# The up product of an MLP as seven products of halves, with the residual kept in DRAM meanwhile

## The chip, the cores and the metric

The program runs on one core of one Trainium2 chip. The metric is the device time of one execution in microseconds (us); of the kernel before, three runs took 4327.98, 4333.91 and 4335.40 us, so the median is 4333.91 us. A profile of one further execution was taken.

The engines by the names that the profile uses: PE multiplies matrices into PSUM, PEld loads its stationary operand, DVE (VectorE) and ACT (ScalarE) work on tiles and may read PSUM, POOL (GpSimd) works on tiles in SBUF alone, SP issues DMAs. ACT issues DMAs as well.

## The reference, cut to what matters

Two layers of a transformer block run on 1024 tokens with 1024 features; a second, larger layer follows them. The end of each of the two layers is the part that changes:

```python
x = x + gate_a * mix                                   # mix = mixed @ w_out
h = rms_norm(x) * (1.0 + scale_f) + shift_f
x = x + gate_f * (jnp.square(jax.nn.relu(h @ w_mlp_up[l])) @ w_mlp_down[l])   # 1024 -> 4096 -> 1024
```

In the second layer's filters, `h @ w4` (64 features, 2 x 512 channels per direction) is multiplied by a decay; that is where the last part of the change is.

## The kernel before, in words

Activations lie transposed: a tile `x[f, hf]` holds 128 features (f of 8) by 512 tokens (hf of 2), and a matmul has 512 columns. All matrix products are in three parts for precision: each fp32 operand is split into a high part (`split_hi`, L194, a copy on ACT that rounds) and a low part (`split_lo`, L200, a subtraction on POOL or DVE), and high*high, high*low and low*high are accumulated in PSUM. A split of a tile of 128x1024 serves a block of weights of 1024x128.

`lighter` (L1317) picks DVE or POOL for a tile operation by adding up fixed costs, 0.60 for DVE and 1.23 for POOL for 512 columns; `plus` (L1326) uses it.

Order of work. The program is written in Python; when it is built, a list scheduler gives every engine one fixed queue. It takes instructions by their place in the program (earlier is more urgent) as soon as its own model of time says that they are ready and a buffer is free. On the chip each engine then works through its queue in that order and waits at each instruction for its semaphores. A buffer tag with `bufs=2` has two tiles in turn; a third must wait until the first is free.

The end of a layer, `layer1` from L559: the output projection (`project_out`, L579) adds `w_out` products to `xa`. Its last part, for the second half of the tokens, runs after the norm of the first half, with 2 PSUM tiles (tag `mm`). `norm` (L291) takes the sum of squares (`presum`, `rstd`) and makes, from each `xa[f, hf]`, a scaled tile (L299, DVE), a shift (ACT) and the split: DVE and ACT for f in 0, 2, 4, 6, 7, and ACT and POOL for f in 1, 3, 5. The split features H (16 tiles, high and low) stay for the up product, and `xa` stays as residual.

`mlp` (L605), up stage: 16 quarters (c of 8, j of 2). A quarter loads two blocks of `w_mlp_up` of 1024x128 (columns 256 apart), splits them, and makes 2 x 2 products of 24 matmuls (`up_part`, L617): 96 matmuls. ACT takes the ReLU out of PSUM (L622), DVE multiplies (L623). `up_store` (L633) writes the four results and, for c < 7, three more combinations (four subtractions on DVE, L640 to L646) to DRAM, on the ACT queue: they are the factors of the down product, which is made already as seven products of halves for c < 7 (`factor`, L688; `multiply`, L720). Its first weights are split before the up stage ends. `gated` (L733) adds to `xa`. Then the next layer's norm begins.

`filter_spectra` (L1500) makes, for pairs of 128 positions, four products in fp32 with 64 rows of the PE: direction b of 2 lies in rows 0 to 63 or 64 to 127 and writes its own PSUM bank, e is the position block. Each product is two matmul instructions. They stand in the order b0 e0, b0 e1, b1 e0, b1 e1.

Of the kernel before, what the change touches and what calls it, by code (L numbers as in the profile page):

```python
# [19 lines left out]
NF = D // 128  # L20
# [127 lines left out]
class Kernel:  # L148
# [319 lines left out]
    def layer1(self, l, state, xclose, enter_next, rclose):  # L468
        nc, i = self.nc, self.i
        _, H, xs, close = state  # L470
# [7 lines left out]
        mixd = self.DR.tile([2, 8, 2, 128, 512], F32, name=f"mix{l}")  # L478
# [4 lines left out]
        tmp, tclose = self.open("mla_tmp", "right")  # L483
# [12 lines left out]
        with self.pool("mod") as p:  # L496
# [14 lines left out]
            for n in range(34):  # L511
                h, i = divmod(n, 8)
# [19 lines left out]
        rclose()  # L532

        xp, xclose = self.open("x", "right")
        xa = {(f, hf): xp.tile([128, 512], F32, name=f"xa{f}_{hf}") for hf in range(2) for f in range(NF)}
        gp0, gclose0 = self.open("gla_in", "right")
        G = self.gla_setup(l, gp0, A)
        self.psum(f"ps_gla{l}")
# [21 lines left out]
        self.psum(f"ps_mlp{l}")  # L560

        mp, mpclose = self.open("mlp", "right")
        hp, hclose = self.open("h2_0")
        hq, hqclose = self.open("h2_1")
        H = {}
        self.h_tiles(H, hp, "f", 0)
        self.h_tiles(H, hq, "f", 1)
        s1 = self.C.tile([128, NF], F32, name=f"s1_f{l}")
        nc.vector.tensor_scalar(s1, scale_f, 1.0, None, op0=ALU.add)
        with self.pool("ntmp2", "left") as tmp:  # L570
            for hf in range(2):
                if hf:
                    self.drain(self.project_out(l, mp, mixd, 0, xa, gate_a, "mm", 2, (hf,)))
                self.norm(tmp, xa, H, s1, shift_f, hf)
        mpclose()
        return self.mlp(l, H, xa, gate_f, lambda: (hqclose(), hclose()), lambda: enter_next(xa, wclose)), xclose

    def project_out(self, l, mp, mixd, part, xa, gate, tag, bufs, halves=(0, 1)):

# [22 lines left out]
        for _ in steps:  # L602
            pass

    def mlp(self, l, H, x, gate, hclose, enter_next):  # L605


        nc, i = self.nc, self.i
        up, down = i["w_mlp_up"][l], i["w_mlp_down"][l]

        actd = self.DR.tile([8, 7, 2, 128, 512], F32, name=f"act{l}")
        dp, dpclose = self.open("mlp_raw", "right")
        sp, spclose = self.open("mlp_sq")

        def square():
            return sp.tile([128, 512], F32, name="square", tag="square", bufs=11)

        def up_part(w, hf):
            ps = self.PS.tile([128, 512], F32, name="up", tag="dn", bufs=4)
            self.gemm(ps, w, slice(0, 128), lambda k, h: H[k, h], 8, hf)  # L620
            sq = square()
            nc.scalar.activation(sq, ps, AF.Relu)  # L622
            nc.vector.tensor_mul(sq, ps, sq)  # L623
            return sq

        def up_weights(c, j):
            return [self.load_w([(up[:, n0 : n0 + 128], 0)], 8, 128, shared="v" if c + j == 0 else False) for n0 in (c * 512 + j * 128, c * 512 + j * 128 + 256)]

        def up_store(c, j, B):

            store = lambda n, t: nc.scalar.dma_start(actd[c, n, j], t)
            if c == 7:
                for n in range(4):  # L633
                    store(n, B[n // 2, n % 2])
                return
            store(0, B[0, 0])
            store(1, B[1, 0])
            store(2, B[1, 1])
            t2, t3, t4 = square(), square(), square()
            nc.vector.tensor_sub(t3, B[1, 1], B[0, 1])  # L640
            store(6, t3)
            nc.vector.tensor_sub(B[0, 1], B[0, 1], B[0, 0])
            store(4, B[0, 1])
            nc.vector.tensor_sub(t2, B[1, 1], B[0, 1])
            store(5, t2)
            nc.vector.tensor_sub(t4, B[1, 0], t2)  # L646
            store(3, t4)

        def raw_a(c, m, k):
# [7 lines left out]
        def raw_b(c, n):  # L657
            t = dp.tile([128, 2, 512], F32, name="sq_raw", tag="sqr", bufs=5)
            nc.sync.dma_start(t, actd[c, n].rearrange("j p n -> p j n"))
            B[c, n] = t  # L660

        turns = {}

        def exact(name, raw, lo_vector=False):

# [53 lines left out]

        def multiply(f, pairs):  # L720

            turns["ps"] = (turns.get("ps", -1) + 1) % 3
            tag, bufs = ("mm", 2) if turns["ps"] == 2 else ("dn", 4)
            ps = self.PS.tile([128, 512], F32, name="dn", tag=tag, bufs=bufs)
            n, last = 0, 6 * len(pairs) - 1
            for (wh, wl), (ah, al) in pairs:
                for j in range(2):
                    for a, b in ((wh, ah), (wh, al), (wl, ah)):
                        self.mm(ps, a[:, j, f * 128 : f * 128 + 128], b[:, j], n == 0, n == last)
                        n += 1  # L730
            return ps
# [2 lines left out]
            nc.vector.scalar_tensor_tensor(x[f, hf], y, gate[:, f : f + 1], x[f, hf], op0=ALU.mult, op1=ALU.add)  # L734

        load = loads()
        for c in range(8):
            for j in range(2):
                w, sq = up_weights(c, j), {}
                if (c, j) == (7, 1):  # L740

                    next(load)
                    next(load)
                    first = factor(0, 0)
                    next(first)
                    next(first)

                for m, hf in ((0, 0), (1, 0), (0, 1), (1, 1)) if c + j == 0 else ((0, 0), (0, 1), (1, 0), (1, 1)):
                    sq[m, hf] = up_part(w[m], hf)
                up_store(c, j, sq)  # L750
        spclose()
        hclose()
        dx, dxclose = self.open("mlp_late", "right")
# [749 lines left out]
    def filter_spectra(self, p, o, g):  # L1503

        nc, n = self.nc, 256
        if o + g == 0:
            self.mats = p.tile([128, 25, 128], F32, name="dftf")
        dec_ = self.k["decay"].rearrange("p (b a c) -> p b a c", b=2, a=8)[:, :, :, g * n : (g + 1) * n]
        ze = p.tile([128, 8, n], F32, name="ze", tag="ze", bufs=1)
        zo = p.tile([128, 8, n], F32, name="zo", tag="zo", bufs=1)  # L1510
        for a in range(0, 8, 2):
            dec = p.tile([128, 2, 2, n], F32, name="decay", tag="decay", bufs=2)
            for b in range(2):
                nc.sync.dma_start(dec[:, b], dec_[:, b, a : a + 2])
            ps = self.PS.tile([128, 2, 2, n], F32, name="f_ps", tag="big", bufs=2)
            for b in range(2):
                P = slice(64 * b, 64 * b + 64)
                for e in range(2):
                    self.mm(ps[:, b, e], self.hid[P, (a + e) * 128 : (a + e + 1) * 128], self.fw4[P, o, g * n : (g + 1) * n], True, True)
                self.load[0] += 0.67  # L1520
                nc.vector.tensor_mul(dec[:, b], ps[:, b], dec[:, b])
            self.plus(ze[:, a : a + 2], dec[:, 0], dec[:, 1])
            self.plus(zo[:, a : a + 2], dec[:, 0], dec[:, 1], ALU.subtract)
        slots = {}

        def Y(d):
            slots[d] = p.tile([128, 2, n], F32, name="Yf", tag="Yf", bufs=4)
            return slots[d]

        def flush(ds):  # L1530
            for d in ds:
# [715 lines left out]
```

## Time and profile before

| what | value |
|---|---|
| median of three runs | 4333.91 us |
| the profiled execution's own time | 4335.62 us |
| its span, first to last instruction | 4333.8 us |
| mean granted clock of PE | 0.963 |
| PE busy | 4008.1 us (92%) |
| DVE, ACT, POOL busy | 2228.9, 1529.8, 1590.5 us |
| up stage, layer 0 and 1 | 713.6 to 1072, 2064.9 to 2421 us |

Busy time is the time in which at least one instruction of the engine is shown; the matmuls overlap (each is shown with some 390 ns, and the next one starts after some 227 ns), so the rate of PE is read from the number of matmuls in a stretch. In a line of a view, `out<-in` names tiles by the program's names.

### The profile page before, as it was taken

The numbers are of one execution on the slowest core, as the hardware profiler recorded it, in microseconds if no ns is written. First come the engines' busy times: TensorE is split into PE (matmuls) and PEld (weight loads), VectorE is DVE, ScalarE is ACT, GpSimd is POOL, SyncE is SP. The second block draws the span as 40 slices with busy tenths as digits, with TensorE's granted clock in tenths as the row PEclk, the third lists the DMA queues.
The fourth block names the chain that finished last, engine by engine and source line by source line (L and its number), as shares of the span: only waits on it lengthen the run. The fifth ranks groups of instructions, "written<-read, shape, count | busy, mean of one in ns | idle before, by whom it ended". The sixth has DMA issues, their size and how long they took to land. (4 is left out here: it accounts for less than half of the span.)

```text
span 4333.8 us, 52750 instructions
## 1 busy us (share of the span) xinstructions
PE 4008.1 (92%) x19412; PEld 3134.3 (72%) x19412; DVE 2228.9 (51%) x3919; ACT 1529.8 (35%) x2774; POOL 1590.5 (37%) x1315
## 2 busy tenths in 40 slices
PE   6999888999999899888999999899999999999698
PEld 3776676888787595566788788567777776778576
DVE  5426686332788516586433477742221444567445
ACT  5425454212433525444311333322223545211222
POOL 3422364222876422165222688212220111334242
PEclk8999899999999999999999999999999999999899
DMA  6245534433442126643433443344454332444363
GB/s 199 61 132 170 161 113 141 162 134 122 161 156 81 48 86 197 193 132 112 161 132 133 151 145 106 108 106 116 117 144 96 98 93 79 143 148 145 127 180 109
DMA packets 634355, 563.12 MB, mean 130 GB/s; under 512 B 202536, under 2 KB 473854, under 8 KB 634098
## 3 DMA queue, kind: packets, MB, share of 16 engines
q1 hardware_dynamic: 412826, 409.31, 31.2%
q10 hardware_dynamic: 220696, 149.27, 10.9%
q8 instruction: 153, 2.51, 0.2%
q0 software_dynamic: 576, 1.18, 0.1%
q14 instruction: 104, 0.85, 0.1%
HBM read 399.49 MB, written 157.54 MB: 129 GB/s over the span
## 5 line engine op out<-in xcount | busy, mean ns | idle before, releaser
L200 POOL TENSOR_TENSOR w_lo<-w_raw,w_hi 128x1024 fp32r<-128x1024 f32 (+4 forms) x237 | 447.7, 1890 | 1458.6 <-ACT w_hi L194 1401.5
L194 ACT ACTIVATE w_hi<-w_raw 128x1024 fp32r<-128x1024 f32 (+4 forms) x276 | 236.6, 859 | 800.7 <-PE in L191 283.4
L191 PE MATMUL in<-b2h,w_hi 128*128 128x512 f32 x1152 | 474.9, 412 | 7.1 <-ACT qkv_t L1794 7.1
L191 PE MATMUL in<-b2l,w_hi 128*128 128x512 f32 x1152 | 460.2, 400 | 0.6 <-POOL b2l L200 0.6
L191 PE MATMUL in<-b2h,w_lo 128*128 128x512 f32 x1152 | 460.5, 400 | 0.0
L191 PE MATMUL up<-fl,w_hi 128*128 128x512 f32 x1024 | 400.3, 391 | 1.9 <-POOL fl L200 1.2
L191 PE MATMUL up<-fh,w_hi 128*128 128x512 f32 x1024 | 400.7, 392 | 0.0
L191 PE MATMUL up<-fh,w_lo 128*128 128x512 f32 x1024 | 400.2, 391 | 0.0
L191 PE MATMUL dn<-b_hi,a_hi 128*128 128x512 f32 x912 | 358.7, 395 | 4.2 <-ACT b_hi L194 2.0
L191 PE MATMUL dn<-b_lo,a_hi 128*128 128x512 f32 x912 | 359.0, 394 | 2.6 <-POOL b_lo L200 2.6
L191 PE MATMUL dn<-b_hi,a_lo 128*128 128x512 f32 x912 | 358.9, 394 | 0.0
L623 DVE TENSOR_TENSOR square<-up,square 128x512 f32<-128x512 f32 x128 | 88.2, 691 | 460.7 <-ACT square L622 452.8
L200 POOL TENSOR_TENSOR a_lo<-dn_raw,a_hi 128x1024 fp32r<-128x1024 f32 x92 | 241.1, 2621 | 119.2 <-ACT a_hi L194 119.0
L191 PEld LDWEIGHTS in<-b2h,w_hi 128*128 128x128 f32 x1152 | 221.6, 192 | 66.7 <-issue 13.1
L191 PEld LDWEIGHTS in<-b2h,w_lo 128*128 128x128 f32 x1152 | 221.2, 192 | 54.1 <-issue 7.3
L191 PEld LDWEIGHTS in<-b2l,w_hi 128*128 128x128 f32 x1152 | 221.5, 192 | 48.5 <-issue 4.4
L200 POOL TENSOR_TENSOR b_lo<-sq_raw,b_hi 128x1024 fp32r<-128x1024 f32 x92 | 239.5, 2604 | 6.2 <-ACT b_hi L194 6.2
L194 ACT ACTIVATE a_hi<-dn_raw 128x1024 fp32r<-128x1024 f32 x106 | 112.6, 1062 | 338.8 <-PE dn L191 118.3
L191 PE MATMUL wo<-mix,w_hi 128*128 128x512 f32 x512 | 185.4, 437 | 43.0 <-DVE xa L598 26.2
L191 PEld LDWEIGHTS up<-fl,w_hi 128*128 128x128 f32 x1024 | 192.9, 188 | 44.3 <-POOL fl L200 2.1
L191 PEld LDWEIGHTS up<-fh,w_hi 128*128 128x128 f32 x1024 | 193.2, 189 | 41.6 <-issue 0.8
L191 PEld LDWEIGHTS up<-fh,w_lo 128*128 128x128 f32 x1024 | 193.1, 189 | 40.5 <-issue 0.5
(505 smaller groups left out, 8721.0 us busy)
## 6 DMA issues: line engine op xcount, KB each, us to landing
wada<-in_w_ada SPq DMA_DIRECT2D x120, 512.0 KB
act<-square ACTq DMA_DIRECT2D x212, 256.0 KB
sq_raw<-act SPq DMA_DIRECT2D x106, 512.0 KB
w_raw<-in_w_in SPq DMA_DIRECT2D x102, 512.0 KB
w_raw<-in_w_mlp_up SPq DMA_DIRECT2D x64, 512.0 KB
dn_raw<-in_w_mlp_down SPq DMA_DIRECT2D x64, 512.0 KB
qkv<-qkv_t ACTq DMA_DIRECT2D x72, 256.0 KB
w_raw<-in_w_out SPq DMA_DIRECT2D x64, 256.0 KB
```

The source lines that it names most:

```text
L191: return self.nc.tensor.matmul(out, lhsT, rhs, start=start, stop=stop, **kw)
L194: self.nc.scalar.activation(hi, x, AF.Copy, **kw)
L200: return eng.tensor_sub(lo, x, hi.bitcast(F32))
L623: nc.vector.tensor_mul(sq, ps, sq)
```

## The change

1. **Up product.** A quarter's weights are taken as blocks a11, a12 (first 128 columns; first and last 512 features) and a21, a22 (second 128 columns), and the features as b11, b21 (first half of the tokens; first and last 512 features), b12 and b22. Sums of blocks are made and split, and seven products of 12 matmuls with 512 features each replace the four of 24: 84 matmuls a quarter. The results are put together by additions out of PSUM on DVE, with one copy on ACT; ReLU and square are one DVE instruction in SBUF. Per quarter the weights need four sums on DVE and six splits (one of 1024 columns, five of 512).
2. **Features.** The normed features are written in place, into `xa`; for the second half of the tokens, 4 x 4 differences and 4 x 5 splits on `lighter`'s choice of DVE or POOL make the factors of the products 2 to 6. 40 tiles stay in `h2`, 16 more lie in the place of `xa`.
3. **Residual.** `xa` is written to DRAM on the ACT queue (16 DMAs per layer) before the norm overwrites it, and read back on SP (16 DMAs) when the places are free, before the down product adds to it.
4. **Differences for the down product.** The four subtractions of `up_store` go from DVE to POOL; results and differences lie in pairs in the buffers of the down stage's `sq_raw` (5 of them).
5. **Order.** The first products of the first two quarters, which need the first half of the tokens alone, stand ahead of all the rest.
6. **Output projection.** Its last part uses 4 PSUM tiles (tag `dn`) in place of 2.
7. **Filters.** The four products of a pair stand in the order e0 b0, e0 b1, e1 b0, e1 b1, held by explicit dependencies.

The core of the diff:

```diff
+        xd = self.DR.tile([NF, 2, 128, 512], F32, name=f"x_mlp{l}")
+        H = {(q, f): [hp.tile([128, 512], F32R, name=f"f{q}{b}{f}") for b in "hl"] for q in (0, 1, 2, 4, 6) for f in range(4)}
+        def exact(q, f, t):
+            self.split_hi(H[q, f][0], t)
+            self.split_lo(H[q, f][1], t, H[q, f][0], True)
         with self.pool("ntmp2", "left") as tmp:
             for hf in range(2):
                 if hf:
-                    self.drain(self.project_out(l, mp, mixd, 0, xa, gate_a, "mm", 2, (hf,)))
-                self.norm(tmp, xa, H, s1, shift_f, hf)
+                    self.drain(self.project_out(l, mp, mixd, 0, xa, gate_a, "dn", 4, (hf,)))
+                r = self.norm_rstd(tmp, xa, hf)
+                for f in range(NF):
+                    nc.scalar.dma_start(xd[f, hf], xa[f, hf])
+                for f in range(4):
+                    for g in (f, 4 + f):
+                        t = xa[g, hf]
+                        nc.vector.scalar_tensor_tensor(t, t, s1[:, g : g + 1], r, op0=ALU.mult, op1=ALU.mult)
+                        nc.scalar.activation(t, t, AF.Identity, bias=shift_f[:, g : g + 1])
+                    if hf == 0:
+                        exact(0, f, xa[f, 0])
+                        exact(1, f, xa[4 + f, 0])
+                        continue
+                    b11, b12, b21, b22 = xa[f, 0], xa[f, 1], xa[4 + f, 0], xa[4 + f, 1]
+                    exact(2, f, b22)
+                    self.plus(t3, b22, b12, ALU.subtract)
+                    exact(6, f, t3)
+                    self.plus(b12, b12, b11, ALU.subtract)
+                    exact(4, f, b12)
+                    self.plus(t2, b22, b12, ALU.subtract)
+                    self.plus(t4, b21, t2, ALU.subtract)
+                    H[5, f] = [place(f, 0, F32R), place(f, 1, F32R)]
+                    exact(5, f, t2)
+                    H[3, f] = [place(4 + f, 1, F32R), place(4 + f, 0, F32R)]
+                    exact(3, f, t4)
...
+        def up_quarter(c, j):
...
+            w0 = pair("w")
+            split(w0, 0, R[0], c + j == 0)
+            p1 = temp("p1", 2)
+            nc.scalar.activation(p1, up_product(0, part(w0, 0)), AF.Copy)
+            c11, c21 = squares()
+            V.tensor_add(c11, up_product(1, part(w0, 1)), p1)
+            V.scalar_tensor_tensor(c11, c11, 0.0, c11, op0=ALU.max, op1=ALU.mult)
+            yield
+            w2 = pair("w")
+            split(w2, 0, a22)
+            V.tensor_add(a22, a21, a22)
+            V.tensor_sub(a21, a11, a21)
+            V.tensor_sub(a11, a22, a11)
+            V.tensor_sub(a12, a12, a11)
+            w1 = pair("a")
+            split(w1, 0, a11)
+            split(w1, 1, a21)
+            split(w2, 1, a22)
+            w3 = pair("w" if last else "b")
+            split(w3, 0, a12)
+            yield
+            V.tensor_add(u2, up_product(5, part(w1, 0)), p1)
+            V.tensor_add(u3, up_product(6, part(w1, 1)), u2)
+            yield
+            V.tensor_add(c21, up_product(3, part(w2, 0)), u3)
+            V.scalar_tensor_tensor(c21, c21, 0.0, c21, op0=ALU.max, op1=ALU.mult)
+            ps = up_product(4, part(w2, 1))
+            V.tensor_add(c22, ps, u3)
+            V.tensor_add(u4, ps, u2)
+            V.scalar_tensor_tensor(c22, c22, 0.0, c22, op0=ALU.max, op1=ALU.mult)
+            V.tensor_add(c12, up_product(2, part(w3, 0)), u4)
+            V.scalar_tensor_tensor(c12, c12, 0.0, c12, op0=ALU.max, op1=ALU.mult)
+            up_store(c, j, {(0, 0): c11, (0, 1): c12, (1, 0): c21, (1, 1): c22})
...
-            t2, t3, t4 = square(), square(), square()
-            nc.vector.tensor_sub(t3, B[1, 1], B[0, 1])
+            (t2, t3), (t4, _) = squares(), squares()
+            minus = nc.gpsimd.tensor_sub
+            minus(t3, B[1, 1], B[0, 1])
...
+        for n in range(2):
+            next(quarters[n])
...
+        for t in (1, 0):
+            for f in range(NF):
+                x[f, t] = place(f, t)
+                nc.sync.dma_start(x[f, t], xd[f, t])
...
+            group = []
+            for e in range(2):
+                for b in range(2):
+                    P = slice(64 * b, 64 * b + 64)
+                    group.append(self.mm(ps[:, b, e], self.hid[P, ...], self.fw4[P, o, ...], True, True))
+            self.in_order(group)
```

The pairs of tag `w` have 2 tiles in turn, `a` and `b` one each.

## Rows read from the trace of the kernel before

**Rows 1.** The page: busy us of each engine, share of the span, instructions.
```profile
PE 4008.1 (92%) x19412; PEld 3134.3 (72%) x19412; DVE 2228.9 (51%) x3919; ACT 1529.8 (35%) x2774; POOL 1590.5 (37%) x1315
```
**Rows 2.** Busy time by stretch: us, each engine's busy us (instructions), clock, DMA share, GB/s.
```profile
740.00:1060.00 320.00, 320.00 (x1414) 264.94 (x1413) 97.29 (x119) 64.89 (x91) 72.03 (x30) 1.00 0.43 144
...
1080.00:1340.00 260.00, 258.51 (x1119) 209.61 (x1120) 196.10 (x213) 102.17 (x108) 219.12 (x86) 1.00 0.45 145
...
713.00:740.00 27.00, 21.95 (x79) 15.72 (x78) 18.01 (x22) 13.51 (x21) 7.02 (x5) 0.87 0.37 124
...
690.00:713.00 23.00, 17.83 (x68) 13.44 (x68) 21.75 (x24) 12.70 (x22) 12.92 (x8) 0.93 0.26 73
...
467.00:500.00 33.00, 24.83 (x97) 18.14 (x96) 14.55 (x25) 16.29 (x22) 6.38 (x15) 0.69 0.81 247
```
**Rows 3.** The page's groups: an up matmul, of three such lines.
```profile
L191 PE MATMUL up<-fl,w_hi 128*128 128x512 f32 x1024 | 400.3, 391 | 1.9 <-POOL fl L200 1.2
```
**Rows 4.** Timeline of DVE and of POOL around one subtraction of up_store.
```profile
2096.44 1.78 DVE L640 TENSOR_TENSOR square<-square 128x512 f32<-128x512 f32 x1
2098.25 0.69 DVE L642 TENSOR_TENSOR square<-square 128x512 f32<-128x512 f32 x1
...
2095.27 2.40 POOL L200 TENSOR_TENSOR w_lo<-w_raw,w_hi 128x1024 fp32r<-128x1024 f32 x1 [1.51 <-ACT w_hi L194]
```
**Rows 5.** Groups by line and shape: operands in SBUF alone, then out of PSUM.
```profile
L640 DVE TENSOR_TENSOR square<-square 128x512 f32<-128x512 f32 x28 | 50.0, 1786 | 1.0
...
L773 DVE TENSOR_TENSOR sum<-dn,sum 128x512 f32<-128x512 f32 x192 | 127.9, 684 | 64.7 <-PE dn L191 64.7
...
L194 ACT ACTIVATE w_hi<-w_raw 128x512 fp32r<-128x512 f32 x80 | 49.7, 624 | 79.5 <-PE wo L191 34.6 <-POOL queries L1051 16.7 <-POOL o_lo L200 12.6
```
**Rows 6.** Timelines of POOL and DVE: operations of one engine back to back.
```profile
703.56 1.27 POOL L200 TENSOR_TENSOR w_lo<-w_raw,w_hi 128x512 fp32r<-128x512 f32 x1
704.79 1.73 POOL L200 TENSOR_TENSOR fl<-nt,fh 128x512 fp32r<-128x512 f32 x1
...
1208.94 2.40 POOL L200 TENSOR_TENSOR b_lo<-sq_raw,b_hi 128x1024 fp32r<-128x1024 f32 x1
1211.31 2.40 POOL L200 TENSOR_TENSOR a_lo<-dn_raw,a_hi 128x1024 fp32r<-128x1024 f32 x1
...
2939.56 1.29 DVE L1521 TENSOR_TENSOR decay<-f_ps,decay 128x512 f32<-128x512 f32 x2 [1.75 <-DMA decay<-const_decay]
```
**Rows 7.** Timeline of DVE in the norm of the second half, layer 0.
```profile
727.14 0.69 DVE L240 SCALAR_TENSOR_TENSOR rstd<-rstd_u,rstd 128x512 f32<-128x512 f32 x1
727.87 2.08 DVE L299 SCALAR_TENSOR_TENSOR nt<-xa,s_f,rstd 128x512 f32<-128x512 f32 x3
...
737.54 2.48 DVE L307 SCALAR_TENSOR_TENSOR fl<-nt,mod,fh 128x512 fp32r<-128x512 f32 x2
```
**Rows 8.** Timeline of PE around the wait for the second half's sum of squares.
```profile
720.78 2.07 PE L191 MATMUL ms<-nacc,ones_d 128*128 128x512 f32 x2 [4.13 <-POOL nacc L1684]
...
723.51 0.63 PE L191 MATMUL up<-fh,w_lo 128*128 128x512 f32 x1
723.93 0.63 PE L191 MATMUL up<-fh,w_hi 128*128 128x512 f32 x1
```
**Rows 9.** Tile xa: the issue of a spill of the residual, duration least/median/most in ns.
```profile
L334 ACTq DMA_DIRECT2D x_spill_a<-xa x16: 326/326/327, 1365.6 to 1397.9; - x16
```
**Rows 10.** Timelines of PE and DVE in the filters.
```profile
2843.58 1.22 PE L191 MATMUL f_ps<-fw,fhid 64*128 64x256 f32 x8
2844.72 0.50 PE L191 MATMUL in<-b2h,w_lo 128*128 128x512 f32 x1
...
2927.39 5.81 PE L191 MATMUL f_ps<-fw,fhid 64*128 64x256 f32 x24
2933.14 0.50 PE L191 MATMUL in<-b2h,w_hi 128*128 128x512 f32 x1
...
2937.11 0.69 DVE L1521 TENSOR_TENSOR decay<-f_ps,decay 128x512 f32<-128x512 f32 x1 [4.06 <-DMA decay<-const_decay]
```

More of the change, by code (lines that the diff above doesn't have):

```diff
@@ L534, in layer1 @@
         xp, xclose = self.open("x", "right")
-        xa = {(f, hf): xp.tile([128, 512], F32, name=f"xa{f}_{hf}") for hf in range(2) for f in range(NF)}
+        place = lambda f, hf, dtype=F32: xp.tile([128, 512], dtype, name="xa", tag=f"xa{f}_{hf}", bufs=1)
+        xa = {(f, hf): place(f, hf) for hf in range(2) for f in range(NF)}
         gp0, gclose0 = self.open("gla_in", "right")
@@ L562, in layer1 @@
         mp, mpclose = self.open("mlp", "right")
[L563 to L567, printed above, removed]
+        hp, hclose = self.open("h2")
+        xd = self.DR.tile([NF, 2, 128, 512], F32, name=f"x_mlp{l}")
+        H = {(q, f): [hp.tile([128, 512], F32R, name=f"f{q}{b}{f}") for b in "hl"] for q in (0, 1, 2, 4, 6) for f in range(4)}
         s1 = self.C.tile([128, NF], F32, name=f"s1_f{l}")
         nc.vector.tensor_scalar(s1, scale_f, 1.0, None, op0=ALU.add)
+        def exact(q, f, t):
+            self.split_hi(H[q, f][0], t)
+            self.split_lo(H[q, f][1], t, H[q, f][0], True)
         with self.pool("ntmp2", "left") as tmp:
@@ L572, in layer1 @@
                 if hf:
-                    self.drain(self.project_out(l, mp, mixd, 0, xa, gate_a, "mm", 2, (hf,)))
-                self.norm(tmp, xa, H, s1, shift_f, hf)
+                    self.drain(self.project_out(l, mp, mixd, 0, xa, gate_a, "dn", 4, (hf,)))
[13 more added lines that the diff above has]
+                    exact(2, f, b22)
+                    t3 = tmp.tile([128, 512], F32, name="nt", tag="nt", bufs=3)
+                    self.plus(t3, b22, b12, ALU.subtract)
+                    exact(6, f, t3)
+                    self.plus(b12, b12, b11, ALU.subtract)
+                    exact(4, f, b12)
+                    t2, t4 = (tmp.tile([128, 512], F32, name="nt2", tag="nt2", bufs=4) for _ in range(2))
+                    self.plus(t2, b22, b12, ALU.subtract)
[4 more added lines that the diff above has]
+                    exact(3, f, t4)
         mpclose()
-        return self.mlp(l, H, xa, gate_f, lambda: (hqclose(), hclose()), lambda: enter_next(xa, wclose)), xclose
+        return self.mlp(l, H, xa, (xd, place), gate_f, hclose, lambda: enter_next(xa, wclose)), xclose
     def project_out(self, l, mp, mixd, part, xa, gate, tag, bufs, halves=(0, 1)):
@@ L603, in drain, with mlp @@
             pass
-    def mlp(self, l, H, x, gate, hclose, enter_next):
+    def mlp(self, l, H, x, xd, gate, hclose, enter_next):
         nc, i = self.nc, self.i
@@ L611, in mlp @@
         actd = self.DR.tile([8, 7, 2, 128, 512], F32, name=f"act{l}")
+        turns = {}
+        xd, place = xd
         dp, dpclose = self.open("mlp_raw", "right")
         sp, spclose = self.open("mlp_sq")
[L615 to L624, printed above, removed]
@@ L626, in up_weights, with psum_tile, temp @@
-        def up_weights(c, j):
-            return [self.load_w([(up[:, n0 : n0 + 128], 0)], 8, 128, shared="v" if c + j == 0 else False) for n0 in (c * 512 + j * 128, c * 512 + j * 128 + 256)]
+        def psum_tile(name):
+            turns["ps"] = (turns.get("ps", -1) + 1) % 3
+            tag, bufs = ("mm", 2) if turns["ps"] == 2 else ("dn", 4)
+            return self.PS.tile([128, 512], F32, name=name, tag=tag, bufs=bufs)
+        def temp(name, bufs=1):
+            return sp.tile([128, 512], F32, name=name, tag=name, bufs=bufs)
@@ new lines, in squares, with up_product, split @@
+        def squares():
+            t = dp.tile([128, 2, 512], F32, name="squares", tag="sqr", bufs=5)
+            return t[:, 0], t[:, 1]
+        def up_product(q, w):
+            ps = psum_tile("up")
+            n = 0
+            for k in range(4):
+                hh, hl = H[q, k]
+                for a, b in ((w[0], hh), (w[0], hl), (w[1], hh)):
+                    self.mm(ps, a[:, k], b, n == 0, n == 11)
+                    n += 1
+            return ps
+        def split(t, at, raw, vector=False):
+            at = slice(4 * at, 4 * at + raw.shape[1])
+            self.split_hi(t[0][:, at], raw)
+            self.split_lo(t[1][:, at], raw, t[0][:, at], "v" if vector else False)
@@ new lines, in pair, with part @@
+        def pair(place):
+            pool, tag, bufs = (self.W, "", 2) if place == "w" else (dp, place, 1)
+            return [pool.tile([128, 8, 128], F32R, name=f"w_{b}", tag=f"w{b[0]}{tag}", bufs=bufs) for b in ("hi", "lo")]
+        def part(t, at):
+            return [x[:, 4 * at : 4 * at + 4] for x in t]
+        def up_quarter(c, j):
+            V = nc.vector
+            R = []
+            for m in range(2):
+                R.append((self.W if m else dp).tile([128, 8, 128], F32, name="w_raw", tag="wr" if m else "dnr", bufs=2 if m else 4))
+                n0 = c * 512 + j * 128 + m * 256
+                nc.sync.dma_start(R[m], up[:, n0 : n0 + 128].rearrange("(k p) n -> p k n", p=128))
+            a11, a12, a21, a22 = (R[m][:, 4 * k : 4 * k + 4] for m in range(2) for k in range(2))
+            last = (c, j) == (7, 1)
+            w0 = pair("w")
[19 more added lines that the diff above has]
+            yield
+            u2, u3, u4 = temp("u2"), temp("u3"), temp("u4")
+            c22, c12 = squares()
+            V.tensor_add(u2, up_product(5, part(w1, 0)), p1)
[10 more added lines that the diff above has]
+            up_store(c, j, {(0, 0): c11, (0, 1): c12, (1, 0): c21, (1, 1): c22})
@@ L638, in up_store @@
             store(2, B[1, 1])
-            t2, t3, t4 = square(), square(), square()
-            nc.vector.tensor_sub(t3, B[1, 1], B[0, 1])
+            (t2, t3), (t4, _) = squares(), squares()
+            minus = nc.gpsimd.tensor_sub
+            minus(t3, B[1, 1], B[0, 1])
             store(6, t3)
-            nc.vector.tensor_sub(B[0, 1], B[0, 1], B[0, 0])
+            minus(B[0, 1], B[0, 1], B[0, 0])
             store(4, B[0, 1])
-            nc.vector.tensor_sub(t2, B[1, 1], B[0, 1])
+            minus(t2, B[1, 1], B[0, 1])
             store(5, t2)
-            nc.vector.tensor_sub(t4, B[1, 0], t2)
+            minus(t4, B[1, 0], t2)
             store(3, t4)
@@ L660, in raw_b @@
             B[c, n] = t
-        turns = {}
         def exact(name, raw, lo_vector=False):
@@ L720, in multiply @@
         def multiply(f, pairs):
-            turns["ps"] = (turns.get("ps", -1) + 1) % 3
-            tag, bufs = ("mm", 2) if turns["ps"] == 2 else ("dn", 4)
-            ps = self.PS.tile([128, 512], F32, name="dn", tag=tag, bufs=bufs)
+            ps = psum_tile("dn")
             n, last = 0, 6 * len(pairs) - 1
@@ L736, in mlp @@
         load = loads()
[L737 to L750, printed above, removed]
+        quarters = [up_quarter(c, j) for c in range(8) for j in range(2)]
+        for n in range(2):
+            next(quarters[n])
+        for n in range(16):
+            if n == 15:
+                next(load)
+                next(load)
+                for _ in range(3):
+                    next(quarters[n])
+                first = factor(0, 0)
+                next(first)
+                next(first)
+            self.drain(quarters[n])
+        for t in (1, 0):
+            for f in range(NF):
+                x[f, t] = place(f, t)
+                nc.sync.dma_start(x[f, t], xd[f, t])
         spclose()
@@ L1515, in filter_spectra @@
             ps = self.PS.tile([128, 2, 2, n], F32, name="f_ps", tag="big", bufs=2)
+            group = []
+            for e in range(2):
+                for b in range(2):
+                    P = slice(64 * b, 64 * b + 64)
+                    group.append(self.mm(ps[:, b, e], self.hid[P, (a + e) * 128 : (a + e + 1) * 128], self.fw4[P, o, g * n : (g + 1) * n], True, True))
+            self.in_order(group)
             for b in range(2):
-                P = slice(64 * b, 64 * b + 64)
-                for e in range(2):
-                    self.mm(ps[:, b, e], self.hid[P, (a + e) * 128 : (a + e + 1) * 128], self.fw4[P, o, g * n : (g + 1) * n], True, True)
                 self.load[0] += 0.67
```

## The prediction

> **What bounds the kernel now.** I read the page first: PE is busy 4008.1 of 4333.8 us, no other engine over 52% [rows 1]. Then busy time by stretch: between 740 and 1060 us, inside the up stage, PE starts 1414 matmuls in 320 us and never idles, so one matmul costs 0.2263 us there; POOL is busy 72 us and DVE 97 us of the 320 [rows 2]. The reader is to see that the shown 391 ns of a matmul [rows 3] are not its price. Third, the timelines around the up stage's start, because there PE waits for tiles (21.95 us busy in the 27 us from 713, at a clock of 0.87 [rows 2]). Last, what DVE and POOL do to each other, since the change moves most of its new work to these two.
>
> **The port.** A subtraction of two SBUF tiles on DVE takes 0.69 us alone, but 1.78 us when POOL is at work on two SBUF tiles: POOL's operation from 2095.27 ends at 2097.67 and DVE's from 2096.44 ends at 2098.22, 0.55 us later [rows 4]. All 28 of that line take 1786 ns on average, while DVE's additions out of PSUM stay at 684 ns in the down stage, where POOL is busy 219 of 260 us [rows 2, 5]. So I count POOL's operations and those of DVE with two SBUF operands as one shared resource and add their times; DVE operations out of PSUM are free of it. Back to back, 512 columns cost 1.23 us on POOL, 1024 cost 2.37, a DVE subtraction 0.60 [rows 6], a DVE scalar_tensor_tensor 0.67 (three in 2.08 us, the last shown with 0.74) [rows 7].
>
> **Part 1, fewer matmuls.** A quarter goes from 96 to 84 matmuls, from 21.72 to 19.01 us of PE. 16 quarters in 2 layers: 384 x 0.2263 = **-86.9 us**, -43.4 a layer. The down stage keeps its work.
>
> **Part 2, a quarter in its steady state.** On the port stand, per quarter: POOL's split of 1024 columns 2.37, five of 512 and four differences 9 x 1.23 = 11.07; on DVE four weight sums 4 x 0.60 = 2.40 and four ReLU-squares 4 x 0.67 = 2.68. Together 18.5 us of PE's 19.0, where before the port held 2 x 2.37 + 4 x 0.60 = 7.1 of 21.7. DVE's seven additions out of PSUM lie beside it. The capacity just suffices, but the work isn't spread. The split of a22 can begin only when product 4 of the quarter before frees the pair `w`, 2.72 us before the quarter starts; then come the split (0.62 on ACT [rows 5], 1.23 on POOL), three sums (1.80), and the split of a11 (0.62 + 1.23): 5.5 us, done 2.8 us after the quarter starts, against product 5's turn at 5.4 us. In the same stretch the quarter before ends: c12 is added and squared (0.69 + 0.74), and then four differences want POOL for 4.9 us, earlier in the program and so more urgent. All of it ahead of a11's split would make it 8 us, 2.2 us late (1.4 + 4.9 + 1.2 = 7.5, and 0.1 to 0.2 for each change of engine). The queue's order decides; none of it is in the trace. Bounds: 0 to 2.2 us of PE's wait per quarter. I take 0.5, nearer the lower end, because two of the five splits are needed late (products 4 and 2) and PE's queue may put product 3, whose weights are ready, first. 15 x 0.5 = **+7.5 us** a layer.
>
> The four differences were on DVE before. The Trainium skill, GPSIMD Engine Reference, section Engine selection, says to keep elementwise work of two inputs on VectorE, as GpSimd is about twice as slow; 1.23 against 0.60 us here agrees. By that rule these four would leave the port at 16.0 us a quarter and the wait at nothing, so this placement would be the change's own loss of 7.5 us a layer.
>
> **Part 3, the norm of the second half.** Today it takes from 727.87 to 740.0 us [rows 7], 12.2 us, and the first up products cover part. After: 8 scalings (8 x 0.67 = 5.4) and 36 splits and differences, which `lighter`'s costs share 2 to 1: 24 on DVE (14.4) and 12 on POOL (14.8). On the port these add up to 34.5 us; the first quarter's later weights add 5 x 1.23 + 4 x 0.60 = 8.6 if they all fall between. Bounds 34.5 and 43.1; I take the middle, 39: features complete at 727.9 + 39 = 766.9. PE has meanwhile the 48 matmuls on the first half and, as slice by slice becomes ready, three of four slices of five products, 45: 93, where today it has done 73 by 740 (79 starts less 6 that aren't up [rows 2]). So PE loses 26.9 - 20 x 0.2263 = **+22.4 us** a layer. Layer 1 has the same form.
>
> After 4.1 us of idling PE's next matmuls start every 0.42 us, not 0.23, so the granted clock is at its 1.2 GHz level [rows 8]. After this longer wait the last 15 matmuls run so: 15 x 0.2 = 3 us, of which today's stage has a part: **+2** a layer (0 to 4).
>
> **Part 4, smaller ones, per layer.** The 16 spills cost 16 x 0.33 = 5.2 us of ACT [rows 9]; ACT idles 10.3 of the 23 us from 690 [rows 2], which hides them, and the scaling that overwrites `xa` waits anyway for the sum of squares over the same tiles. Without this cover the whole 5.2 would go ahead of the norm; +1. Reading back 16 x 256 KB = 4.2 MB takes 17 us at the 247 GB/s of a stretch with such loads [rows 2]; half may start 10.9 us before the up stage's end, behind product 5, the other half 5.4 us before, behind product 3. SP's queue then has the next raw loads of the down stage behind them. The first addition needs `xa` 5.4 us into the down stage, and six PSUM tiles hold 8 us more; +1 (0 to 10). Four PSUM tiles: between 690 and 713 PE needs 68 x 0.2263 = 15.4 of 23 us [rows 2], so up to 7.6 us lie there, but DVE is busy 21.75 of the 23 and the sum of squares waits for DVE's last addition; -2 (-6 to 0).
>
> **Part 5, filters.** Eight matmul instructions that happened to alternate take 1.14 us, 24 in today's order 5.75, or 1.92 for eight [rows 10]: 0.78 saved in each of 15 tiles, at most 11.7 us. But behind three tiles DVE waits 4.06 us for the decay's DMA [rows 10], so PE mostly arrives early at the same wait; I take **-4** (-11.7 to 0). The Trainium skill, TensorEngine Tiling (Array Packing), section PSUM Bottleneck, says that row tiles speed up the matmul and not the emptying of PSUM; by it this term would be 0 and the sum 4 us higher.
>
> **The sum.** Per layer -43.4 + 7.5 + 22.4 + 2 + 1 + 1 - 2 = -11.5; two layers -23, filters -4: **-27 us**. The profiled execution took 4335.6 us (4333.8 of span and 1.8 around it), so 4308.6; it was 1.7 us above the median of the runs, so I predict 4307 us. Most of what the matmuls save is given back where DVE and POOL share the port.
>
> **Rivals.**
> *A, the port costs little.* The queues interleave well: no wait in the steady quarter (-15), features in 34.5 us (-9), filters at most of their bound (-8): -59, 4275 us. For: 18.5 is less than 19.0, and the down stage has POOL busy 219 of 260 us and PE 258.5 [rows 2]. Against: two chains and an urgent burst per quarter.
> *B, the differences stand ahead of the weights.* On POOL the four differences of a quarter go before the split of a11, so product 5 starts 2.2 us late in each quarter: 15 x 2 x 2.2 = 66 in place of 15: +51, 4358 us, slower. It decides from a wait of 1.4 us a quarter (0.5 + 27/30). For: program order makes them more urgent. Against: PE's queue may hold product 3 in that place.
> *C, the second half's norm takes 52 us* (43 and a gap for each ACT step between two port steps): +13 a layer, 4333 us, no change.
> That parts 6 and 7 of the change do nothing is inside their bounds.
>
> **Chances.** Mine 0.43, its own range 4287 to 4326; A 0.25, B 0.22, C 0.10. The range of 8 in 10 is 4262 to 4360, with A's 4275 and B's 4358 in it. 0.2% (8.7 us) is about what a measurement of this kernel tells from no change. Faster by more: A and nearly all of mine, 0.64; within: C and the upper edge of mine, 0.13; slower: B and a little of C, 0.23.
>
> **What would show it.** 84 matmuls a quarter at 0.226 us, and a quarter of 19.5 us; PE's idle time in the up stage ended by POOL's low parts of the weights (tile `w_lo`); the last low part of the second half some 39 us after the first scaling, with DVE operations of 1.7 us in it; a clock below 1 there. If a quarter takes 19.0 us A is right, at 21.2 us B. It is wrong as a whole if PE waits elsewhere, above all for `xa` at the down stage's start.

## The result: slower by 1.2%, and the profile after

The changed kernel takes 4381.12 us (median of four runs, 4377.76 to 4384.22) against 4331.11 for the kernel before on the same chip: 1.0119 times, 95% interval 1.0104 to 1.0133. The prediction was 4307 us, faster, with a range up to 4360: wrong in sign and outside its range. The page's line of busy time, and PE's waits from 700 to 1100 us (us in total, times, longest):

```profile
PE 3923.3 (90%) x19028; PEld 3054.0 (70%) x19028; DVE 2490.8 (57%) x4196; ACT 1565.6 (36%) x2850; POOL 1931.2 (44%) x1574
```

```profile
PE up L191 <- ACT w_hi L194: 38.4, 2, 37.5
PE up L191 <- POOL w_lo L200: 22.5, 14, 1.6
```

PE has 85 us less to do than in [rows 1], as planned; the two waits, which the kernel before hardly had, cost more. Where they lie shows in the windows (us, then busy us and instructions of PE, PEld, DVE, ACT, POOL, granted clock, DMA share, GB/s):

```profile
840.00:1060.00 220.00, 203.77 (x874) 162.93 (x874) 137.52 (x159) 48.14 (x74) 154.64 (x103) 1.00 0.40 135
690.00:720.00 30.00, 20.50 (x76) 14.75 (x74) 18.21 (x23) 15.51 (x27) 12.83 (x9) 0.89 0.42 130
720.00:760.00 40.00, 2.41 (x6) 1.13 (x5) 33.93 (x35) 19.95 (x32) 19.21 (x12) 0.51 0.06 16
```

In the steady stage PE was never idle before [rows 2]; now it is busy 204 of 220 us. And between 720 and 760 us it starts four matmuls (the row's six count two that began before 720), a time in which the kernel before was well into its first products and from 740 us on never idle [rows 2].

**The start of the up stage.** Timelines of PE, SP, ACT and DVE; the last fence is what SP's queue waited for (us, times, longest):

```profile
719.34 1.12 PE L191 MATMUL ms<-nacc,ones_d 128*128 128x512 f32 x2 [2.40 <-POOL nacc L1792]
758.02 0.80 PE L191 MATMUL up<-f0h,w_hi 128*128 128x512 f32 x1 [37.55 <-ACT w_hi L194]
...
759.87 0.63 PE L191 MATMUL up<-f0h,w_hi 128*128 128x512 f32 x1
760.30 0.63 PE L191 MATMUL up<-f0l,w_hi 128*128 128x512 f32 x1
...
709.56 50.59 SPq L692 DMA_DIRECT2D w_raw<-in_w_mlp_up  x6
...
756.39 0.63 ACT L194 ACTIVATE xa<-nt 128x512 fp32r<-128x512 f32 x1 [1.15 <-POOL nt L1432]
756.93 1.04 ACT L194 ACTIVATE w_hi<-w_raw 128x1024 fp32r<-128x1024 f32 x1
...
724.06 2.74 DVE L586 SCALAR_TENSOR_TENSOR xa<-xa,s_f,rstd 128x512 f32<-128x512 f32 x4
729.66 1.75 DVE L200 TENSOR_TENSOR f6l<-nt,f6h 128x512 fp32r<-128x512 f32 x1
755.34 2.40 DVE L200 TENSOR_TENSOR xa<-nt,xa 128x512 fp32r<-128x512 f32 x2
758.00 1.23 DVE L200 TENSOR_TENSOR w_lo<-w_raw,w_hi 128x1024 fp32r<-128x1024 f32 x1 [0.25 <-ACT w_hi L194]
```

```profile
SPq L692 <- DVE xa L586: 36.1, 1, 36.1
```

The split of the first weights in the kernel before, ACT's high part and DVE's low part:

```profile
710.77 1.06 ACT L194 ACTIVATE w_hi<-w_raw 128x1024 fp32r<-128x1024 f32 x1 [2.42 <-PE wo L191]
...
712.07 1.22 DVE L200 TENSOR_TENSOR w_lo<-w_raw,w_hi 128x1024 fp32r<-128x1024 f32 x1
```

The norm of the second half lasts from 724.06 to 757.74: 33.7 us. All that time PE has nothing, though the features of the first half are ready: the split of the first weights, high part at 756.93 and low part at 758.00, stands behind the whole norm on ACT and DVE. In the kernel before it was done at 713.29, well ahead of the first scaling at 727.87 [rows 7]. The load itself waited 36.1 us for a scaling of the norm. In the compiled program the first raw block of quarter 0, which the change took from the pool `self.W` into a pool opened after the norm, lies at bytes 143328 to 147424 of each partition and the norm's `rstd` from 147136: the scaling is rstd's last reader. PE's matmuls from 759.87 start 0.43 us apart, the 1.2 GHz level; the granted clock of the window from 720 to 760 is 0.51.

**A steady quarter** now takes 21.26 us from first matmul to first matmul, 21.76 before. Timelines of POOL, DVE and ACT where PE waits for a11's low part:

```profile
909.13 3.00 POOL L200 TENSOR_TENSOR w_lo<-w_raw,w_hi 128x512 fp32r<-128x512 f32 x2 [1.89 <-ACT w_hi L194]
912.76 1.67 POOL L743 TENSOR_TENSOR squares<-squares 128x512 f32<-128x512 f32 x1 [0.63 <-DVE squares L728]
914.38 1.26 POOL L200 TENSOR_TENSOR w_lo<-w_raw,w_hi 128x512 fp32r<-128x512 f32 x1
...
910.90 1.78 DVE L728 SCALAR_TENSOR_TENSOR squares<-squares 128x512 f32<-128x512 f32 x1
...
911.01 0.63 ACT L194 ACTIVATE w_hi<-w_raw 128x512 fp32r<-128x512 f32 x1 [1.16 <-DVE w_raw L707]
```

a11's high part is ready at 911.64, but its low part starts at 914.38: the first difference of the quarter before (L743) stands ahead of it in POOL's queue, and waits itself for the square of c12 (L728).

### The profile page after: what moved, and what is told of

Its sections match the earlier page's. It is cut to its first block, busy times and chain, and to the rows that moved or that the text cites. A ratio compares the mean times of both kernels' runs of the same rounds, so it can differ in the third digit from the quotient of the medians.

```text
span 4381.4 us, 52855 instructions
## 1 busy us (share of the span) xinstructions
PE 3923.3 (90%) x19028; PEld 3054.0 (70%) x19028; DVE 2490.8 (57%) x4196; ACT 1565.6 (36%) x2850; POOL 1931.2 (44%) x1574
## 5 line engine op out<-in xcount | busy, mean ns | idle before, releaser
L200 POOL TENSOR_TENSOR w_lo<-w_raw,w_hi 128x512 fp32r<-128x512 f32 (+4 forms) x367 | 595.8, 1633 | 1179.5 <-ACT w_hi L194 1114.5
L194 ACT ACTIVATE w_hi<-w_raw 128x512 fp32r<-128x512 f32 (+4 forms) x404 | 300.7, 752 | 1079.1 <-PE in L191 275.3
L191 PEld LDWEIGHTS dn<-b_hi,a_hi 128*128 128x128 f32 x912 | 171.5, 188 | 48.4 <-issue 4.5
L191 PEld LDWEIGHTS dn<-b_lo,a_hi 128*128 128x128 f32 x912 | 171.4, 188 | 43.6 <-POOL b_lo L200 4.7
L191 PEld LDWEIGHTS dn<-b_hi,a_lo 128*128 128x128 f32 x912 | 171.5, 188 | 39.4 <-POOL a_lo L200 0.4
L200 DVE TENSOR_TENSOR w_lo<-w_raw,w_hi 128x1024 fp32r<-128x1024 f32 (+1 forms) x37 | 40.7, 1100 | 236.2 <-ACT w_hi L194 236.0
L877 DVE TENSOR_TENSOR sum<-dn,sum 128x512 f32<-128x512 f32 x192 | 128.0, 684 | 65.2 <-PE dn L191 65.2
L191 PE MATMUL up<-xa,w_hi 128*128 128x512 f32 x512 | 160.2, 394 | 1.7 <-ACT w_hi L194 1.7
L191 PEld LDWEIGHTS wo<-mix,w_hi 128*128 128x128 f32 x512 | 103.7, 209 | 78.5 <-ACT w_hi L194 23.3
```

Of the source, the lines that this page charges most:

```text
L191: return self.nc.tensor.matmul(out, lhsT, rhs, start=start, stop=stop, **kw)
L194: self.nc.scalar.activation(hi, x, AF.Copy, **kw)
L200: return eng.tensor_sub(lo, x, hi.bitcast(F32))
L877: nc.vector.tensor_add(acc[q, f], ps, acc[q, f])
```

## The experiments

All edits are to the changed kernel unless it says otherwise.

**1. The differences on VectorE again** (`minus_vector`).

```diff
-            minus = nc.gpsimd.tensor_sub
+            minus = nc.vector.tensor_sub
```

> Only change against the kernel after: the four differences of up_store on VectorE again. Theory (GpSimd's queue with the differences ahead of a11's low part, and the port taken by them, costs 2.24 us in each quarter): quarter 21.25 -> 19.2 to 19.6 us, 28 steady quarters x 1.8 = -50, total 4331 (4322 to 4342). Rival (VectorE becomes late in its turn, since its queue then holds four more operations of 0.7 to 1.7 us ahead of a quarter's evictions): quarter 20.5 us or more, total 4360 or more.

Measured: 4338.91 us, ratio to the kernel before 1.0017 (1.0006 to 1.0027), quarter 19.44. PE never idles in the window:

```profile
800.00:1060.00 260.00, 260.00 (x1126) 209.92 (x1125) 220.30 (x255) 62.01 (x93) 132.31 (x79) 1.00 0.47 155
```

So 42 of the 50 us lost hang on where these four operations stand. The theory's number holds; whether it is the queue or the port, this run can't tell.

**2. Differences on GpSimd, but later** (`minus_late`): the stores of a quarter are written behind the splits of the next.

```diff
             split(w3, 0, a12)
+            if done:
+                done.pop()()
             yield
...
-            up_store(c, j, {(0, 0): c11, ...})
+            done.append(lambda: up_store(c, j, B))     # c < 7
```

> The differences stay on GpSimd, but the stores of a quarter are written after the next quarter's splits, so that all five split operations of a quarter stand ahead of the first difference in GpSimd's queue. If the place in the queue is the cause: no wait of PE for a11's low part, quarter 19.0 to 19.8 us, total 4325 to 4345. If it is the port, which the differences take from VectorE wherever they stand: quarter 20.5 to 21.3 us, total 4362 to 4381.

Measured: 4360.48 us, ratio 1.0071 (1.0054 to 1.0088); quarter 20.27, between the two expectations. ACT's timeline with its DMA issues (ACTq), then the last difference on POOL:

```profile
920.47 7.49 ACTq L739 DMA_DIRECT2D act<-squares  x6
...
928.06 0.63 ACT L194 ACTIVATE w_hi<-w_raw 128x512 fp32r<-128x512 f32 x1 [9.68 <-DVE squares L726]
...
925.50 1.61 POOL L755 TENSOR_TENSOR squares<-squares 128x512 f32<-128x512 f32 x1
```

The ACTIVATE is the split of a22. Its buffer came free at 926.98, when PE left product 4, but ahead of it in ACT's queue stood the stores, the last of them that of a difference which POOL ended at 927.11; ACT issued it until 927.96. A difference that is later on POOL makes ACT's queue late, because ACT issues the stores.

**3. As 2, with those stores issued by SyncE** (`late_other_queue`, one run).

```diff
-            store = lambda n, t: nc.scalar.dma_start(actd[c, n, j], t)
+            store = lambda n, t: (nc.scalar if c == 7 or n < 3 else nc.sync).dma_start(actd[c, n, j], t)
```

> minus_late, with the stores of the four differences issued by SyncE in place of ScalarE; the differences stay on GpSimd. Theory (in minus_late the quarter of 20.27 us is held by ScalarE's queue: the split of a22 idles 9.68 us behind stores that wait for the late differences): quarter 19.4 to 19.7 us, no wait of PE for a low part of over 5 us in the whole stage, total some 20 us under minus_late's 4360. Rival (what is left, 0.8 us per quarter, is the port that the differences take from VectorE wherever they and their stores stand): quarter 20.1 to 20.4 us.

Measured: 4328.0 us (4328.78 for the kernel before beside it), quarter 19.44:

```profile
800.00:1060.00 260.00, 260.00 (x1125) 210.04 (x1124) 177.03 (x203) 63.28 (x96) 205.40 (x134) 1.00 0.45 151
```

POOL still does all four differences (busy 205 of 260 us, 132 in experiment 1), and PE never idles. The port has room for this work, as Part 2 had counted; the cost was the order in two queues.

**4. a11's low part alone on VectorE** (`a11_vector`, one run): `split(w1, 0, a11, True)`.

> The kernel after, with the low part of a11 alone on VectorE; differences on GpSimd and where they were. Theory (PE waits in each quarter for that low part because one difference stands ahead of it in GpSimd's queue): quarter 19.4 to 19.9 us, total 4340 to 4352. Rival (the port: on VectorE it waits out the differences as well): quarter 20.5 us or more, total 4362 or more.

Measured: 4374.81 us, quarter 20.59: the rival's number. Timelines of POOL and DVE:

```profile
914.08 1.67 POOL L743 TENSOR_TENSOR squares<-squares 128x512 f32<-128x512 f32 x1 [0.62 <-DVE squares L728]
...
914.53 1.77 DVE L200 TENSOR_TENSOR w_lo<-w_raw,w_hi 128x512 fp32r<-128x512 f32 x1
```

Out of POOL's queue, the low part still meets the same difference, at the port: it ends 0.55 us after it, as in [rows 4], and takes 1.77 in place of 0.60 [rows 6]; the quarter exceeds 19.44 by 1.15 us. The Trainium skill, "SBUF — State Buffer", section Who interferes with whom, says that a VectorE instruction with two SBUF inputs contends with a GpSimd instruction that reads SBUF, and that the shared port pair is an exclusive lock; this pair of rows agrees. One operation ahead of a11's split was the cost, by queue or by port.

**5. First weights out of the norm's memory and ahead of its queue** (`first_in_norm`): the raw blocks of quarters 0 and 1 swap pools (R[0] into `self.W`), `squares` lies below them, one buffer of `nt` fewer.

```diff
+            c11, c21 = squares()          # ahead of R
...
+                w = m if c or j > 1 else 1 - m
-                R.append((self.W if m else dp).tile(...
+                R.append((self.W if w else dp).tile(...
```

> The differences stay on GpSimd; only the place of the first two quarters' raw weights changes (R[0] of quarters 0 and 1 in self.W, R[1] in the raw pool, squares ahead of them in memory, one buffer of nt fewer). Theory (PE idles 38 us per layer because the first weights lie under the norm's temporaries and their splits are queued behind the norm): the four products on the first half, 48 matmuls of 0.2263 us = 10.9 us, run while the norm of the second half runs; the idle stretch ahead of the up stage falls from 38.1 to 26 to 28 us in each layer, quarters stay at 21.2 us, total 4381 - 20 = 4361 (4356 to 4366). Rival (the norm is what ends late, and products beside it only lengthen it, by their splits and by what they take of ACT and DVE): the last low part moves from 757.7 to 765 or later, total 4373 to 4385.

Measured: 4383.25 us, ratio 1.0118 (1.0101 to 1.0134): nothing gained, the rival's number. The products did run early (first one at 721.65), and PE then idled 33.43 us. DVE, then PE:

```profile
732.16 0.75 DVE L239 SCALAR_TENSOR_TENSOR rstd_u<-ms,eps,rstd_u 128x512 f32<-128x512 f32 x1 [10.01 <-ACT rstd_u L238]
...
765.01 2.40 DVE L200 TENSOR_TENSOR xa<-nt,xa 128x512 fp32r<-128x512 f32 x2
767.33 1.28 DVE L701 TENSOR_TENSOR squares<-up,p 128x512 f32<-128x512 f32 x2
...
771.62 1.73 DVE L706 TENSOR_TENSOR w_raw<-w_raw 128x512 f32<-128x512 f32 x1 [1.81 <-POOL w_lo L200]
...
774.79 0.80 PE L191 MATMUL up<-f6h,w_hi 128*128 128x512 f32 x1 [33.43 <-ACT w_hi L194]
```

The norm ends at 767.4, but PE gets weights only at 774.8: evictions, a22's split and the sums of the weights come first. In the changed kernel the same chain lay behind the 48 products on the first half (10.9 us); here these were already spent. And the splits, which waited for their loads ahead of the sum of squares on ACT and POOL, delayed rstd: 10.8 us from DVE's last `wo` addition (721.41) to L239, 6.4 in the changed kernel. **My theory that the products were simply missing from the gap fell.** With experiment 1 on top (`both`) it was the same:

> Both edits. Theory (two separate causes that add up): -20 and -50 from 4381, total 4311 (4302 to 4322), which is faster than the kernel before by some 0.5%. Rival (the two hide each other, or either fails by itself): 4331 or more.

Measured: 4340.92 us, ratio 1.0025 (1.0012 to 1.0038), no better than experiment 1 alone.

**6. The place in memory alone** (`place_alone`, one run): experiment 5 without the swap.

> Against the kernel after: only the place in memory; the first quarters' raw weights no longer lie under rstd and nt2. Theory A (the wait of the load for that memory is what keeps PE idle): load of quarter 0 issued at 712 in place of 748.9, first product at 724 or so, total 4361. Theory B (the splits are also written behind the norm in ScalarE's and VectorE's order, so an early load alone changes nothing): load early, split of quarter 0 still at 755 to 758, first product at 756 to 758, total 4376 to 4386.

Measured: 4376.98 us; theory B. SP's loads, ACT's split, PE's first product:

```profile
714.70 11.43 SPq L693 DMA_DIRECT2D w_raw<-in_w_mlp_up  x6
...
762.04 1.99 ACT L194 ACTIVATE w_hi<-w_raw 128x1024 fp32r<-128x1024 f32 x2
...
763.13 0.79 PE L191 MATMUL up<-f0h,w_hi 128*128 128x512 f32 x1 [37.55 <-ACT w_hi L194]
```

The load no longer waits, and PE's idle 37.55 us are the same to the last digit: the order of ACT's and DVE's queues holds it by itself. The memory by itself would have held the load for its 36.1 us. Why the split keeps its place behind the norm in these queues, though its load is early, no run shows.

**7. The norm's second half all on VectorE** (`norm_vector`, on top of experiment 1).

```diff
-            self.split_lo(H[q, f][1], t, H[q, f][0], True)
+            self.split_lo(H[q, f][1], t, H[q, f][0], True if q < 2 else "v")
-                    self.plus(t3, b22, b12, ALU.subtract)      # and b12, t2, t4
+                    nc.vector.tensor_sub(t3, b22, b12)
```

> Against minus_vector (4339): the differences and low parts of the second half's norm, 11 of which stood on GpSimd, all on VectorE. Theory (the 33.7 us of that norm are the sum of what VectorE's and GpSimd's two-operand work takes of a port that they can't use together: 33 operations of 0.62 us and 11 of 1.2 us): 44 x 0.62 = 27.3 us, PE's idle stretch ahead of the up stage 38 -> 32 us in each layer, total 4327 (4323 to 4331). Rival (the chain VectorE, ScalarE, VectorE of each tile sets the norm's length, not the port): norm 32 us or more, total 4336 to 4342.

Measured: 4324.79 us, ratio 0.9994 (0.9980 to 1.0008). The norm runs from 730.34 to 757.99, 27.65 us against 27.3 expected:

```profile
730.34 2.74 DVE L586 SCALAR_TENSOR_TENSOR xa<-xa,s_f,rstd 128x512 f32<-128x512 f32 x4
...
757.30 0.69 DVE L200 TENSOR_TENSOR xa<-nt,xa 128x512 fp32r<-128x512 f32 x1 [0.16 <-ACT xa L194]
```

Twelve operations moved to the busier engine made the norm 6 us shorter (32.6 to 27.7 us in layer 1): DVE and POOL had simply taken turns.

**8. The first quarter's weights made ready before the norm** (`early`, on top of 7): a pool of their own for the raw blocks of quarters 0 and 1, opened ahead of the norm, and quarter 0's splits and sums written ahead of it, on VectorE; one buffer of `nt` fewer.

```diff
+        ep, epclose = self.open("mlp_first", "right")
         mp, mpclose = self.open("mlp", "right")
+        first = [self.up_raw(l, n, (ep, ep)) for n in range(2)]
...
                     self.drain(self.project_out(l, mp, ...))
+                    mpclose()
+                    dq, dqclose = self.open("mlp_pairs", "right")
+                    first[0] = first[0], self.up_first(first[0], dq)   # loads, w0 to w3
```

> Against norm_vector: the raw weights of quarters 0 and 1 lie in a pool of their own, opened before the norm; quarter 0's splits and sums are written ahead of the second half's norm and stand on VectorE. Theory (the 48 products on the first half are worth their 10.9 us only if the chain of sums and splits behind them, some 10 us, is done during the norm too; in first_in_norm it was not, and splits that waited for their loads delayed rstd by 5 us): PE idle ahead of the first product that needs the second half 32 -> 20 to 24 us, total 4327 - 2 x 10 = 4307 (4298 to 4318). Rival (VectorE is full from the last wo product to the end of the norm, so that what is put there lengthens the norm by as much): total 4323 to 4335.

Measured: 4304.6 us, ratio 0.9948 (0.9927 to 0.9969): faster than both kernels. The window of that gap, and the end of the norm on DVE:

```profile
722.00:763.00 41.00, 29.08 (x77) 16.27 (x75) 39.42 (x58) 24.69 (x40) 10.76 (x5) 0.73 0.13 38
```

```profile
762.67 0.68 DVE L200 TENSOR_TENSOR xa<-nt,xa 128x512 fp32r<-128x512 f32 x1
```

PE now starts 75 matmuls in the 41 us (the row's 77 count two that began before), at a clock of 0.73: the 48 on the first half and then 24 of products 6 and 5 as each feature becomes ready, the picture of Part 3. And rstd is not delayed: 6.9 us from the last `wo` addition. The norm itself takes 32.4 us (730.97 to 763.35) in place of 27.65, with the next weights' splits on POOL beside it. The first down product starts at 1060.2 us, 1072.2 before and 1097.4 in the changed kernel.

**9. The filters' order alone, in the kernel before** (`before_filters`).

> The kernel before, with the order of the filters' products alone changed. Theory (the stretch from the down stage's end to the last f_ps product fell by 7.1 us in the changed kernel because of this order): 4331 - 7 = 4324 (4320 to 4328). Rival (the fall belongs to the stretch's start, or is given back behind it): 4329 to 4334.

Measured: 4323.74 us, ratio 0.9993 (0.9977 to 1.0009): inconclusive by the time. PE's waits in that stage, first in the kernel before, then here:

```profile
PE dft_ps L191 <- DVE Yf L1328: 9.9, 3, 4.7
PE f_ps L191 <- DVE decay L1521: 9.3, 6, 2.4
```

```profile
PE dft_ps L191 <- DVE Yf L1328: 24.9, 3, 9.6
PE f_ps L191 <- DVE decay L1524: 1.9, 3, 0.6
```

The waiting for DVE's multiplications, which free the PSUM tiles, fell from 9.3 to 1.9 us; 15.0 us more were waited for the next transform's input. From the down stage's end to the last `f_ps` product this execution takes 443.3 us, the kernel before 457.3 and the changed kernel 450.3; but it was 9 us faster than the median of its own runs. In all eleven traces with the new order this stretch takes 442.0 to 450.3 us, less than in the one trace with the old order. By the times the order is worth 4 us, with an interval from 10 gained to 4 lost, so its size stays open.

## Why the prediction was wrong

By its own parts, in us per layer (layer 0 / layer 1 where they differ), from the first and last matmuls of each stage:

| part | predicted | measured | how measured |
|---|---|---|---|
| 1, fewer matmuls | -43.4 | -37.1 | 16 x (21.76 - 19.44) |
| 2, steady quarter | +7.5 | +23.7 | 13 quarters x (21.26 - 19.44) |
| 3 and 4, norm, clock, spills, PSUM tiles | +23.4 | +38.8 / +37.8 | up stage's start 44.5 / another 39.4 later, first quarters' loss 5.7 / 1.6 smaller |
| 4, read-back | +1 | +1.7 / -0.3 | length of the down stage |
| 5, filters (once) | -4 | -7.1 | down stage's end to the last `f_ps` |
| behind it (once) | 0 | +3.8 | to the end of the span |

The measured column gives 27.1 + 24.1 - 7.1 + 3.8 = +47.9; the spans differ by 47.6. The +3.8 was not followed up. Executions differ too: with the same code ahead of it, the second half's norm starts at 724.06 us here and at 729.17 in experiment 1, so the row of the norm holds to some 5 us. No run takes the spills or the PSUM tiles alone.

**The step that failed first is Part 3's cover**, "PE has meanwhile the 48 matmuls on the first half and ... 45: 93". The norm itself was no worse than forecast: 33.7 us, where I took 39 and had the sum of the port's work, 34.5, as the lower bound. But PE did none of the 93 in that time. I took "ready features" for "ready products" and did not ask where the weights of these products come from: their place was moved by the change, and the queues of ACT and DVE put their split behind the norm (experiment 6). The wider error is that cover counts once. The 48 matmuls also hid the chain of sums and splits behind them, so running them earlier gave nothing (5); with that chain early too, and loads that no longer held up rstd, the cover worked (8). The 15 slow matmuls of the clock term stood in no row: after the wait eight start at the lower level, to 762.01, where the kernel before had nine, to 726.47, so this term was about 0.

**The second is Part 2's 0.5 us**, "0 to 2.2 us of PE's wait per quarter. I take 0.5". The quarter became 1.82 us longer than without the wait, 1.6 of it shown as PE's wait (in [rows 2] there was none): near the upper end, rival B's mechanism, and its mark "at 21.2 us B" was met. (The upper bound is itself off: 8 us less product 5's 5.4 are 2.6, not 2.2.) Its detail was off: not all four differences stood ahead of a11's split but one, and it was enough, since it waits for the square and drags the low part with it. The port alone, which I had as the cause, had room (3). The Trainium skill, "GPSIMD Engine Reference", section Engine selection, which I had weighed, advises VectorE for this work; experiment 1 agrees by 42 us, while 3 keeps the work on GpSimd and is as fast in the quarter.

**Part 1 was mis-sized by 6.3 us a layer.** A matmul of the new stage costs 19.44 / 84 = 0.2314 us, not the 0.2263 taken from [rows 2] (21.76 / 96 = 0.2267 by the quarter), though PE never idles. The down stage had shown it: 258.51 us busy for 1119 matmuls, 0.2310 each [rows 2]. In experiment 1's steady quarters starts are on average 227 ns apart in products 0 and 1 and 231 to 234 in the others. No run here says why.

Right were: neither PE nor DVE waits for the read-back of `xa` at the down stage's start (in layer 1 PE waits 1.6 us for an addition that stood in DVE's queue behind sums of late weights); DVE's operations of 1.75 us in the norm; the low clock there; that reading the residual back costs next to nothing. B and Part 3's loss came together, which no case of mine had: rival B at 4358 kept Part 3's own forecast, and the further 2 x 15 us here and 2 x 6 in Part 1 put the result beyond the range.

## What to carry to other kernels

Work that covers a wait can be spent once: before moving it ahead, list what it covers now, and move that chain with it. For a product to be early, its operands' loads, their place in memory and their operations in each engine's fixed queue must all be early; here the place held the load for 36.1 us and the queues' order held the split by itself, so freeing the place alone showed nothing. When an operation changes engine, look at which queue it enters, what stands behind it there, and whose queue issues the DMA that waits for it.

## What the hardware showed beyond that

DVE's and POOL's work on pairs of SBUF tiles added up without overlap: a norm with 32 such operations on DVE and 12 on POOL took 33.7 us, about the sum of their single times (34.5), and with the 12 on DVE as well 27.65 us. And the pace of back-to-back matmuls of one shape differed by 2% (0.2267 and 0.2314 us) at a granted clock of 1.00 with PE shown busy throughout.
